# Two-layer backbone kernel: other operand sources, order and issue times in the second MLP products, and other PSUM tiles in the passages

## Chip, cores and metric

The kernel runs on one core of one Trainium2 chip. The metric is the device time of one launch in microseconds. Engines: PE (TensorE, matmuls), DVE (VectorE), ACT (ScalarE), POOL (GpSimd), SP (SyncE, which issues most DMAs here).

## What is computed

Two layers over 1024 latent tokens and a prefix of 256 context tokens, width 1024, all in fp32. Layer 0 mixes tokens with windowed attention, layer 1 with bidirectional gated linear attention (GLA); each is followed by an MLP with 4096 hidden units. Only the latent stream of layer 1 is returned, so layer 1's MLP works on latent tokens alone.

```python
def channel_mlp(h, w_in, w_out):
    return jnp.square(jax.nn.relu(h @ w_in)) @ w_out
...
x_lat = x_lat + m_lat[2] * rms_norm(y_lat, g_post_mix[i])
f_lat = channel_mlp(modulate(x_lat, g_pre_mlp[i], m_lat[3], m_lat[4]), w_mlp_in[i], w_mlp_out[i])
x_lat = x_lat + m_lat[5] * rms_norm(f_lat, g_post_mlp[i])
```

## The kernel before

A product of two fp32 operands is three matmuls: each operand is split into a high and a low part (`split`, L212: an ACT cast, then a DVE subtraction), and `mm3` runs high by high (L229), high by low (L230) and low by high (L231). Both matrices of each MLP product are cut in quarters and multiplied with seven products (numbered 1 to 7) in place of eight; sums and differences of quarters are the operands of products 3 to 7, and part of them are made on DVE.

The first product (`mlp_hidden`, L841) runs over 16 units m of hidden rows: for each it loads two column blocks of `w_mlp_in` (`wi`), runs the seven products into the PSUM tiles `pa`, `pb`, `pc`, takes relu and square on ACT into `h`, and `put` (L944) stores `h` to DRAM (`hd`), 512 KB twice per m; `put_x` (L947) stores the context part `hx` of layer 0 in the same way. `x.ops` holds the split activations, `o1h`, `o1l` to `o7h`, `o7l`.

The second product (`mlp_out`, L991) runs twice, once per half kh of the hidden rows, over seven products k in the order 1, 6, 7, 4, 5, 3, 2, eight units j each, and within these over pairs p of token tiles, five with the context (layer 0), four without (layer 1). `fetch` loads one quarter of hidden rows and one of weights, 256 KB each; for k = 6 it loads two of each, for k = 7 nothing, since `sums` makes product 7's operands out of product 6's loads. `sums` makes the operands on DVE: four sums for k = 6, two for 5, one each for 4 and 3. `apart` splits them into `oh` and `ol`. `product` is one triple of matmuls into `p` (or `px`, context), `read` adds the bank to an accumulator `acc`.

The order around the change is set by hand: a `Timeline` holds closures with due times in nominal us, and runs them by time. A fetch is due 9 us ahead of the sums, these 4.5 us ahead of the matmul, the split 3.6 us. A scheduler then places the instructions of each engine, which run in that order. SP issues its DMAs in order too, so a store that waits for its data holds up the loads behind it. All 128 x 1024 tiles come from one SBUF pool of 45 slots. PSUM has four tiles of one bank (`ps1`) and two of two banks (`ps2`).

Between two stages lies a passage, in which token tiles are normalised, transposed on PE and evicted (`modulated`, L430): ACT and DVE take turns on eight 128 x 128 pieces, into `h` or the raw quarters `q`. While `self.tight` is set, the transposes go into one two-bank tile, since the four single banks hold the accumulators of the second product; the tile's first half is evicted before its second half is transposed. For layer 0 a closure sets it just before the second product; for layer 1 (L1841) it is set at once, when the rest of the passage is still in the timeline. The tile `pb` of the first product lies in the two-bank pool as well.

At the end of GLA, `gla_forward` yields a chunk of 128 tokens, `gla_out` normalises it on ACT, POOL and DVE into `on`, and `turn` (L1500) transposes it into `oT` and splits it. `gate_rows` (L407) makes the row `grow` that the residual is scaled with.

Of the kernel before, what the change touches and what calls it, by code (L numbers as in the profile page):

```python
# [11 lines left out]
F32 = mybir.dt.float32  # L12
# [153 lines left out]
class Backbone:  # L166
# [263 lines left out]
    def modulated(self, xn, l, which, s, dst=(), put=None):  # L430

        nc = self.nc
        G, S = self.pre[l, which]
        both = self.ps2("xt") if self.tight else None
        for q in range(2):
            pt = both[:, 512 * q : 512 * (q + 1)] if self.tight else self.ps1("xt")
            for k in range(4):
                kk = 4 * q + k
                nc.tensor.transpose(pt[:, P * k : P * (k + 1)], xn[:, P * kk : P * (kk + 1)], self.ident)
            h = None if put else self.half("h").rearrange("p (k t) -> p k t", k=4)  # L440
            for k in range(4):
                kk = 4 * q + k
                to = put(kk) if put else h[:, k, :]
                src = pt[:, P * k : P * (k + 1)]
                sc, sh = G[:, s, kk : kk + 1], S[:, s, kk : kk + 1]
                if k % 2 == 0:
                    nc.scalar.activation(to, src, AF.Identity, scale=sc, bias=sh)
                else:
                    nc.vector.tensor_scalar(to, src, sc, sh, ALU.mult, ALU.add)
            for k0, k1, hi, lo in dst:  # L450
                a, b = max(k0, 4 * q), min(k1, 4 * q + 4)
                if a < b:
                    self.split(h[:, a - 4 * q : b - 4 * q, :], hi[:, a - k0 : b - k0, :], lo[:, a - k0 : b - k0, :])
# [377 lines left out]
    def hidden_store(self, ctx):  # L831

        lat = [self.dp.tile([P, 2, 512], F32, name=self.nm("hd")) for _ in range(HID // P)]
        if not ctx:
            return lat, None
        return lat, {
# [4 lines left out]
    def mlp_hidden(self, tl, t0, x, store, g):  # L841
# [102 lines left out]
        def put(m, a):  # L944
            nc.sync.dma_start(store[0][2 * m + a], st[m]["h", a])

# [15 lines left out]
        for m in range(n):  # L962
# [28 lines left out]
    def mlp_out(self, tl, t0, l, pairs, store, split_last, done):  # L991
# [10 lines left out]
        step = mm * np_  # L1002
        order = (1, 6, 7, 4, 5, 3, 2)
        when, t = {}, t0
        for kh in range(2):
            for k in order:
                for j in range(8):
# [8 lines left out]
        def unit(s):  # L1016
            return self.u((P, 2, 512), s=s)

        def hid(dst, m, q):
            r, a = quarter[q]  # L1020
            nc.sync.dma_start(dst, lat_store[2 * m + a][:, r, :])

        def wgt(dst, m, q):
# [4 lines left out]
        def fetch(kh, k, j):  # L1028
            m = 8 * kh + j
            if k == 6:  # L1030
                k3[m], raw[k, m] = unit("k3"), unit("wh")
# [14 lines left out]
        def sums(kh, k, j):  # L1046
            m = 8 * kh + j
            tt = nc.vector.tensor_tensor
            if k == 6:
                a, b, r = k2[m], k3[m], raw.pop((k, m))  # L1050
# [13 lines left out]
        def apart(kh, k, j):  # L1064
            m = 8 * kh + j
            src = k2[m] if k in (1, 6) else k3[m] if k == 7 else raw[k, m]
            hi, lo = (self.u((P, 2, 512), F32R, "o" + x) for x in "hl")
# [49 lines left out]
        def read(kh, k, p):  # L1117
# [11 lines left out]
            if kh == 1:  # L1129
                what = {5: "whole", 3: "half", 2: "whole"}.get(k)  # L1130
                if what:
                    done(what, i, acc[i] if what == "half" else acc.pop(i))

        for kh in range(2):
            for n, k in enumerate(order):
                for j in range(8):
# [9 lines left out]
                    if k != 7:  # L1146
                        tl.at((t if k == 1 else ts) - 9, lambda kh=kh, k=k, j=j: fetch(kh, k, j))
                    if k not in (1, 7, 2):
# [9 lines left out]
                if ctx:  # L1158
                    t = when[kh, k, 0]
                    tl.at(t - 14, lambda kh=kh, k=k: cfetch(kh, k))  # L1160
                    if k in (6, 5, 3):
                        tl.at(t - 7, lambda kh=kh, k=k: csums(kh, k))
                    tl.at(t - 4.6, lambda kh=kh, k=k: capart(kh, k))
        return {k: when[1, k, 0] for k in order}, when[1, 2, 8 - split_last], end

# [349 lines left out]
    def run(self):  # L1515
# [253 lines left out]
        row = self.gate_rows(1, 0, 0)  # L1769
        x3d = [self.dp.tile([P, D], F32, name=f"x3d{i}") for i in range(NL_T)]  # L1770
# [10 lines left out]
        def mlp1_ready(left):  # L1781
# [4 lines left out]
            lat, mixed, wo, x2_in, lambda i: row, lambda i: x3d[i - NC_T], h3, 1,  # L1786
            mixed(NC_T), x2_in(NC_T), mlp1_ready,
        )
# [51 lines left out]

        self.tight = True  # L1841
        ts, tp, te = self.mlp_out(tl, t1, 1, pairs, store, 5, spaced)
# [48 lines left out]
```

## Time and profile before

| | us |
|---|---|
| median of three runs | 2640.89 (2640.38 to 2645.94) |
| profiled execution | 2643.85 |
| its span on the core | 2642.1, mean granted PE clock 0.989 |
| attention and layer 0's mixer | 0 to 640 |
| layer 0, first product | 640 to 1054 |
| layer 0, second product and passage | 1054 to 1470 |
| GLA | 1470 to 1893 |
| output projection of layer 1 | 1893 to 1997 |
| layer 1, first product | 1997 to 2312 |
| layer 1, second product | 2312 to 2633 |

The profile's page gives busy time per engine over the whole span. Where a stage loses time is read from windows of the trace, from the waits of one engine in a window (the instruction that waited, and the one that released it), and from timelines.

### The profile page before, as it was taken

What the parts mean: (1) busy time and instruction counts of PE and PEld (TensorE: products, weight loads), DVE (VectorE), ACT (ScalarE), POOL (GpSimd) and SP (SyncE); (2) the same over time, 40 slices, a digit from 0 to 9 for tenths busy, and PEclk for the clock granted to TensorE, in tenths of its full rate; (3) what the DMA queues carried; (4) which work ended last, traced back from release to release, by engine and by line L of the source; (5) the groups of instructions that cost most, each with busy time, mean ns of one, the idle gap of its engine ahead of it and who ended that gap; (6) DMA issues with size and microseconds to landing.
All of it is one profiled execution on the core that took longest, in us unless ns stands there. A gap on an engine that the chain in (4) does not pass through costs nothing.

```text
span 2642.1 us, 36265 instructions
## 1 busy us (share of the span) xinstructions
PE 2561.1 (97%) x13523; PEld 2124.1 (80%) x13523; DVE 1713.7 (65%) x2663; ACT 1258.3 (48%) x2364; POOL 426.3 (16%) x736
## 2 busy tenths in 40 slices
PE   7999999999999999999998999999998999999998
PEld 6777888888888888788876888888786888878787
DVE  4787766657766665766768534736648444478776
ACT  3325777745644444442335444434435555545333
POOL 0355655411000000000001112212310000000002
PEclk9999999999999999999998999999999999999999
DMA  9221000222455575657245222002222343366464
GB/s 308 93 67 41 4 2 20 70 88 84 144 160 160 173 226 179 223 170 233 100 165 194 96 72 69 25 24 96 88 89 64 112 121 102 125 242 213 169 215 167
DMA packets 223520, 329.75 MB, mean 125 GB/s; under 512 B 23896, under 2 KB 122480, under 8 KB 223344
## 3 DMA queue, kind: packets, MB, share of 16 engines
q1 hardware_dynamic: 220752, 318.00, 37.5%
q0 software_dynamic: 2592, 9.44, 0.9%
q8 instruction: 106, 1.74, 0.3%
q14 instruction: 70, 0.57, 0.1%
HBM read 267.60 MB, written 59.77 MB: 124 GB/s over the span
## 4 chain that ended last, share of the span: by engine, by line
PE 85%; DVE 6%; DMA 4%; ACT 2%; issue 1%; POOL 1%; SPq 1%; DVEq 0%; POOLq 0%; ACTq 0%
PE p L229 7%; PE p L230 7%; PE p L231 7%; PE pa L230 4%; PE pa L231 4%; PE pa L229 4%; PE o L760 3%; PE pt L741 3%; PE y L231 3%; PE y L230 2%; PE y L229 2%; PE rp L229 2%; PE rp L230 2%; PE rp L231 2%; PE pc L229 2%; PE pc L231 2%
## 5 line engine op out<-in xcount | busy, mean ns | idle before, releaser
L230 PE MATMUL p<-ol,oh 128*128 128x512 f32 x896 | 351.0, 392 | 1.5 <-DVE ol L214 1.5
L231 PE MATMUL p<-oh,ol 128*128 128x512 f32 x896 | 346.9, 391 | 0.0
L229 PE MATMUL p<-oh 128*128 128x512 f32 x896 | 332.5, 394 | 6.0 <-DVE acc L1125 4.4
L242 POOL TENSOR_SCALAR rs<-ss 128x1 f32<-128x1 f32 (+1 forms) x78 | 25.4, 326 | 1664.4 <-ACT later L236 1483.7
L229 PEld LDWEIGHTS p<-oh 128*128 128x128 f32 x896 | 169.5, 189 | 43.4 <-issue 4.1
L230 PEld LDWEIGHTS p<-ol,oh 128*128 128x128 f32 x896 | 169.6, 189 | 38.8 <-DVE ol L214 2.8
L231 PEld LDWEIGHTS p<-oh,ol 128*128 128x128 f32 x896 | 169.3, 189 | 35.6 <-issue 0.2
L214 DVE TENSOR_TENSOR ol<-wh,oh 128x1024 fp32r<-128x1024 f32 x128 | 153.7, 1216 | 53.8 <-ACT oh L213 50.8
L311 DVE SCALAR_TENSOR_TENSOR ma<-wm,cT,ma 128x1024 f32<-128x1024 f32 x112 | 148.9, 1361 | 55.1 <-DMA wm<-in_w_mod 55.1
L213 ACT CAST oh<-wh 128x1024 fp32r<-128x1024 f32 x128 | 132.4, 1053 | 107.9 <-PE p L231 46.4
L213 ACT CAST oh<-k 128x1024 fp32r<-128x1024 f32 x96 | 98.5, 1054 | 150.8 <-DMA k<-in_w_mlp_out 56.1
L214 DVE TENSOR_TENSOR wi<-wi,wi 128x512 fp32r<-128x512 f32 x176 | 115.4, 685 | 48.1 <-ACT wi L213 46.4
L932 ACT COPY s<-pa 128x512 f32<-128x512 f32 x96 | 55.9, 583 | 183.6 <-PE pa L231 183.5
L936 DVE TENSOR_TENSOR s<-pc,s 128x512 f32<-128x512 f32 x64 | 43.9, 687 | 145.7 <-ACT s L932 135.9
L708 DVE CUSTOM_DVE_ANT_0 pr<-sc,mask,nsink 128x640 f32<-128x640 f32 (+2 forms) x144 | 108.5, 775 | 43.0 <-PE sc L697 41.1
L214 DVE TENSOR_TENSOR ol<-k,oh 128x1024 fp32r<-128x1024 f32 x96 | 115.5, 1218 | 25.6 <-ACT oh L213 16.9
L713 ACT ACTIVATE pr<-pr,nm 128x640 f32<-128x640 f32 (+2 forms) x160 | 118.5, 742 | 28.1 <-DVE nm L708 25.0
L725 POOL TENSOR_SCALAR pr<-pr,den 128x640 f32<-128x640 f32 (+2 forms) x160 | 117.7, 748 | 36.5 <-PE pt L741 16.9
L213 ACT CAST wi<-wi 128x512 fp32r<-128x512 f32 x176 | 102.3, 614 | 39.4 <-DMA hd<-h 25.1
L231 PE MATMUL y<-woh,ol 128*128 128x512 f32 x288 | 113.1, 393 | 2.8 <-DVE ol L214 2.8
L229 PE MATMUL y<-woh,oh 128*128 128x512 f32 x288 | 114.5, 398 | 0.0
L230 PE MATMUL y<-wol,oh 128*128 128x512 f32 x288 | 113.0, 393 | 0.0
(372 smaller groups left out, 6828.5 us busy)
## 6 DMA issues: line engine op xcount, KB each, us to landing
wm<-in_w_mod SPq DMA_DIRECT2D x96, 512.0 KB, 4.6
wh<-hd SPq DMA_DIRECT2D x160, 256.0 KB, 3.8
wh<-in_w_mlp_out SPq DMA_DIRECT2D x160, 256.0 KB, 4.0
wi<-in_w_mlp_in SPq DMA_DIRECT2D x64, 512.0 KB, 5.6
hd<-h SPq DMA_DIRECT2D x64, 512.0 KB, 3.6
k<-hd SPq DMA_DIRECT2D x64, 256.0 KB, 5.3
k<-in_w_mlp_out SPq DMA_DIRECT2D x64, 256.0 KB, 5.3
x<-in_x SPq DMA_DIRECT2D x16, 512.0 KB, 3.6
```

Source lines behind the costliest of these rows:

```text
L213: self.nc.scalar.copy(hi, src)
L214: self.nc.vector.tensor_tensor(lo, src, hi.bitcast(F32), op=ALU.subtract)
L229: mm(out, a[0], b[0], start=start, stop=False, skip_group_check=onto)
L230: mm(out, a[0], b[1], start=False, stop=False, skip_group_check=onto)
L231: mm(out, a[1], b[0], start=False, stop=stop, skip_group_check=onto)
L311: nc.vector.scalar_tensor_tensor(acc[s], raw, c, acc[s], ALU.mult, ALU.add)
L708: nc.vector.tensor_tensor_reduce(out=like(pr), in0=like(ps[e][:, off:768]), in1=mask, scale=1.0, scalar=self.nsink[:, c0 + e : c0 + e + 1] ...
L713: nc.scalar.activation(pr, pr, AF.Exp, bias=nm[:, e : e + 1], scale=-1.0, accum_out=sums[:, e : e + 1])
L725: nc.gpsimd.tensor_scalar(probs[e], probs[e], den[:, e : e + 1], 0.0, ALU.mult, ALU.add)
L741: nc.tensor.transpose(pt[:, P * j : P * (j + 1)], probs[e][:, P * kt : P * (kt + 1)], self.ident)
L760: nc.tensor.matmul(po[64 * e : 64 * (e + 1), P * i4 : P * (i4 + 1)], self.kv[tile_i // 2][:, tile_i % 2, 256 + HD * g : 256 + HD * (g + 1) ...
L932: nc.scalar.copy(s["s", j], s["pa"])
```

## The change

- Layer 1's `put` now makes operands as well. Per m it writes seven units of 256 KB (h11, h11 - h21, h12, h22, and the operands of products 6, 5 and 3) with four DVE sums. The second product loads an operand as it is (`op`); only the weight side is summed there: two sums for k = 6, one for 4 and 5. Product 7 now has a load of its own, product 6 three.
- Layer 0's first half opens with product 2: its order is 2, 1, 6, 7, 4, 5, 3. The second half and layer 1 keep theirs.
- In the second half of either layer, loads, sums and splits of products 4, 5, 3 and 2 are due 2, 5, 9 and 13 us earlier. The loads of product 6 are due earlier, except in layer 1's first half. The context's loads and splits are due 2 to 2.4 us earlier, its sums 2.
- In `modulated` with `tight` set, both halves are transposed before any eviction.
- In layer 1 `tight` is set by a closure one nominal us before the second product.
- The gate row and the first turned tile are written inside GLA's loop, at the third-last and second-last chunk.

```diff
@@ modulated
+        if self.tight:
+            both = self.ps2("xt")
+            for q in range(2):
+                pts[q] = both[:, 512 * q : 512 * (q + 1)]
+                turn(q)
         for q in range(2):
+            if not self.tight:
+                pts[q] = self.ps1("xt")
+                turn(q)
@@ mlp_hidden, put
+            h = st[m]["h", a]
+            if a == 0:
+                nc.vector.tensor_tensor(h[:, 1, :], h[:, 0, :], h[:, 1, :], op=ALU.subtract)
+                nc.sync.dma_start(store[0][m][:, 0:2, :], h)
+                return
+            nc.sync.dma_start(store[0][m][:, 2:4, :], h)
+            h0, s12, s4 = st[m]["h", 0], self.u((P, 2, 512), s="h"), self.u(s="h")[:, :512]
+            nc.vector.tensor_tensor(s12[:, 0, :], h[:, 1, :], h0[:, 1, :], op=ALU.subtract)
+            nc.vector.tensor_tensor(s12[:, 1, :], s12[:, 0, :], h0[:, 0, :], op=ALU.add)
+            nc.vector.tensor_tensor(s4, h[:, 0, :], s12[:, 0, :], op=ALU.subtract)
+            nc.sync.dma_start(store[0][m][:, 4:6, :], s12)
+            nc.sync.dma_start(store[0][m][:, 6, :], s4)
...
-            tl.at(max(at[m, 4], at[m, 3]) + 8, lambda m=m: put(m, 0))
-            tl.at(max(at[m, 3], at[m, 5]) + 8, lambda m=m: put(m, 1))
+            done = max(at[m, 4], at[m, 3], at[m, 5]) + 8
+            tl.at(done, lambda m=m: put(m, 0))
+            tl.at(done, lambda m=m: put(m, 1))
@@ mlp_out
-        order = (1, 6, 7, 4, 5, 3, 2)
+        made = ctx_store is None
+        last = (1, 6, 7, 4, 5, 3, 2)
+        orders = last if made else (2, 1, 6, 7, 4, 5, 3), last
...
+            if made:
+                if k == 6:
+                    b, a, r = k2[m][:, 1, :], k3[m][:, 1, :], raw.pop((1, m))[:, 1, :]
+                    tt(a, b, a, op=ALU.subtract)
+                    tt(b, a, r, op=ALU.add)
+                else:
+                    r = raw[k, m][:, 1, :]
+                    tt(r, r, k2[m][:, 1, :], op=ALU.subtract)
+                return
...
+        leads = {4: 2.0, 5: 5.0, 3: 9.0, 2: 13.0}
...
-                    ts = t - 4.5
+                    ahead = leads.get(k, 0) if kh else 0
+                    ts = t - 4.5 - ahead
+                    tf = ts - 4.5
                     if k == 6:
-                        ts = when[kh, 1, 0] + (1.35 * j + 0.6) * step
+                        t1 = when[kh, 1, 0]
+                        ts = t1 + (1.35 * j + 0.6) * step
+                        tf = ts - 9 if made and not kh else t1 - 9 + (1.25 * j - (3.5 if kh else 1.5)) * step
...
-                    tl.at(t - 3.6, lambda kh=kh, k=k, j=j: apart(kh, k, j))
+                    tl.at(t - 3.6 - ahead, lambda kh=kh, k=k, j=j: apart(kh, k, j))
@@ run, layer 1
+            if i == NT - 3:
+                row = self.gate_rows(1, 0, 0)
+            if i == NT - 2:
+                ready["o"] = self.turn(on[NC_T])
...
-        self.tight = True
+        tl.at(t1 - 1, lambda: tighten(True))
```

How rows stand, at three places. First SP where layer 0's second product opens (`hd` and `in_w_mlp_out` loads fill one tile in turn; `hc` are the context's stores). Before:

```order
L1021 DMA k_2001_10748<-hd_6196 128x512
L1026 DMA k_2001_10748<-in_w_mlp_out 128x512
L949 DMA hc_6229<-hx_10679 128x128
L949 DMA hc_6233<-hx_10679 128x128
L945 DMA hd_6224<-h_10435 128x1024
L1021 DMA k_2005_10772<-hd_6196 128x512
L1026 DMA k_2005_10772<-in_w_mlp_out 128x512
L1021 DMA wh_10773<-hd_6197 128x512
L1026 DMA wh_10773<-in_w_mlp_out 128x512
L1021 DMA k_2007_10778<-hd_6198 128x512
L1026 DMA k_2007_10778<-in_w_mlp_out 128x512
L949 DMA hc_6231<-hx_10817 128x128
```

Now:

```order
L1052 DMA wh_10748<-hd_6197 128x512
L1060 DMA wh_10748<-in_w_mlp_out 128x512
L975 DMA hc_6229<-hx_10678 128x128
L975 DMA hc_6233<-hx_10678 128x128
L958 DMA hd_6224<-h_10435 128x1024
L1052 DMA wh_10776<-hd_6199 128x512
L1060 DMA wh_10776<-in_w_mlp_out 128x512
L975 DMA hc_6231<-hx_10811 128x128
L1052 DMA wh_10826<-hd_6201 128x512
L1060 DMA wh_10826<-in_w_mlp_out 128x512
L975 DMA hc_6235<-hx_10811 128x128
```

Ahead of the last two `hc` stores four tiles' loads (`k`, `wh`) became two, and each j has one tile, of product 2, in place of three.

Second ACT at the end of GLA, where `grow` is the gate row, `on` the squares of a chunk and `woh` the weight's high part. Before:

```order
L1492 ACTIVATE on_17231,ss_3097_17232<-o_2832_15934 128x256 x2
L1492 ACTIVATE on_17231,ss_3097_17232<-oo_17222 128x256 x2
L213 CAST woh_17246<-wor_17244 128x1024
L1492 ACTIVATE on_17262,ss_3106_17263<-o_2832_15934 128x256 x2
L1492 ACTIVATE on_17262,ss_3106_17263<-oo_17253 128x256 x2
L213 CAST woh_17277<-wor_17275 128x1024
L416 COPY grow_17281<-grow_17282 128x512
L416 COPY grow_17281<-grow_17285 128x512
L213 CAST oh_17328<-oT_17330 128x512
L213 CAST oh_17328<-oT_17337 128x512
```

Now:

```order
L416 COPY grow_17205<-grow_17206 128x512
L416 COPY grow_17205<-grow_17209 128x512
L1556 ACTIVATE on_17238,ss_3100_17239<-o_2832_15934 128x256 x2
L1556 ACTIVATE on_17238,ss_3100_17239<-oo_17229 128x256 x2
L213 CAST woh_17253<-wor_17251 128x1024
L213 CAST oh_17257<-oT_17259 128x512
L213 CAST oh_17257<-oT_17266 128x512
L1556 ACTIVATE on_17285,ss_3113_17286<-o_2832_15934 128x256 x2
L1556 ACTIVATE on_17285,ss_3113_17286<-oo_17276 128x256 x2
L213 CAST woh_17300<-wor_17298 128x1024
L213 CAST oh_17330<-oT_17332 128x512
L213 CAST oh_17330<-oT_17339 128x512
```

The gate's copies moved from behind the last chunk's squares to ahead of the last two chunks, the first tile's casts (`oh`) ahead of the last chunk's.

Third PE in layer 1's passage, between products 1 (`pa`, `o1`) and 2 (`pb`, `o2`). Before:

```order
L230 MATMUL pa_18212<-o1l_17878,wi_3277_18145 128x512
L231 MATMUL pa_18212<-o1h_17877,wi_3277_18145 128x512
L439 MATMUL xt_18161<-ident,xn_18083 128x128 x4
L439 MATMUL xt_18225<-ident,xn_18182 128x128 x4
L229 MATMUL pb_18254<-o2h_18122,wi_3283_18189 128x512
L230 MATMUL pb_18254<-o2l_18123,wi_3283_18189 128x512
L231 MATMUL pb_18254<-o2h_18122,wi_3283_18189 128x512
L229 MATMUL pb_18254<-o2h_18122,wi_3283_18189 128x512
```

Now:

```order
L229 MATMUL pa_18197<-o1h_17861,wi_3261_18129 128x512
L230 MATMUL pa_18197<-o1l_17862,wi_3261_18129 128x512
L231 MATMUL pa_18197<-o1h_17861,wi_3261_18129 128x512
L439 MATMUL xt_18210<-ident,xn_18167 128x128 x4
L229 MATMUL pb_18288<-o2h_18106,wi_3277_18235 128x512
L230 MATMUL pb_18288<-o2l_18107,wi_3277_18235 128x512
L231 MATMUL pb_18288<-o2h_18106,wi_3277_18235 128x512
L229 MATMUL pb_18288<-o2h_18106,wi_3277_18235 128x512
```

The two groups of transposes ahead of `pb`, second half of one tile and first half of the next, became one.

## Rows read from the trace of the kernel before

**Rows 1.** The page, part 1: busy time, share of the span, instructions of each engine.

```profile
PE 2561.1 (97%) x13523; PEld 2124.1 (80%) x13523; DVE 1713.7 (65%) x2663; ACT 1258.3 (48%) x2364; POOL 426.3 (16%) x736
```

**Rows 2.** Windows by stage; columns in the first line.

```profile
core 0: us, PE busy (x) PEld busy (x) DVE busy (x) ACT busy (x) POOL busy (x), PEclk, DMA share, GB/s
1054.00:1090.00 36.00, 29.70 (x117) 22.00 (x116) 26.15 (x34) 10.93 (x13) 0.00 (x0) 0.95 0.99 346
1090.00:1396.00 306.00, 305.96 (x1343) 250.20 (x1342) 213.99 (x253) 118.01 (x127) 0.59 (x2) 1.00 0.49 163
1396.00:1470.00 74.00, 65.06 (x277) 52.27 (x277) 58.30 (x84) 41.93 (x75) 13.97 (x21) 0.91 0.43 150
1996.00:2032.00 36.00, 26.67 (x102) 19.69 (x101) 31.00 (x53) 19.76 (x36) 2.21 (x5) 0.86 0.04 15
2032.00:2312.00 280.00, 279.50 (x1231) 230.70 (x1230) 132.01 (x208) 148.67 (x268) 0.00 (x0) 1.00 0.37 113
2312.00:2642.00 330.00, 315.56 (x1382) 258.48 (x1380) 252.68 (x304) 136.60 (x161) 17.09 (x20) 0.99 0.59 201
```

**Rows 3.** PE and ACT waits, opening of layer 0's second product.

```profile
PE px L229 <- ACT oh L213: 6.3, 5, 2.1
...
ACT oh L213 <- DMA k<-in_w_mlp_out: 22.7, 6, 6.7
```

**Rows 4.** Windows of ten us in that opening, columns as in rows 2.

```profile
1070.00:1080.00 10.00, 7.17 (x29) 5.27 (x30) 6.59 (x9) 3.14 (x3) 0.00 (x0) 1.00 0.99 346
1080.00:1090.00 10.00, 7.88 (x29) 6.05 (x28) 8.88 (x11) 3.58 (x5) 0.00 (x0) 0.83 1.05 393
```

**Rows 5.** SP's waits 1020 to 1095, one issue (start, length); the page's cast and landing time.

```profile
SPq L949 <- ACT hx L894: 20.6, 3, 10.0
...
1050.19 0.79 SPq L949 DMA_DIRECT2D hc<-hx  x2
...
L213 ACT CAST oh<-k 128x1024 fp32r<-128x1024 f32 x96 | 98.5, 1054 | 150.8 <-DMA k<-in_w_mlp_out 56.1
...
k<-in_w_mlp_out SPq DMA_DIRECT2D x64, 256.0 KB, 5.3
```

**Rows 6.** PE waits 1395.8 to 1471; one group of eight transposes (start, length).

```profile
PE xt L439 <- DVE h L449: 4.3, 2, 2.4
PE px L229 <- ACT oh L213: 2.1, 2, 1.5
PE p L230 <- DVE ol L214: 1.5, 1, 1.5
...
1447.64 1.03 PE L439 MATMUL xt<-ident,xn 128*128 128x128 f32 x8
```

**Rows 7.** PE waits 1890 to 1898.

```profile
PE y L231 <- DVE ol L214: 2.8, 1, 2.8
PE oT L1506 <- ACT grow L416: 2.3, 1, 2.3
```

**Rows 8.** Windows with the clock low, columns as in rows 2.

```profile
1420.00:1425.00 5.00, 5.00 (x17) 3.88 (x15) 3.94 (x5) 1.41 (x4) 2.82 (x4) 0.58 0.27 108
1898.00:1903.00 5.00, 5.00 (x16) 3.95 (x15) 1.16 (x2) 0.00 (x0) 0.00 (x0) 0.66 0.01 3
2011.00:2018.00 7.00, 4.79 (x11) 3.80 (x12) 3.15 (x8) 0.49 (x2) 0.00 (x0) 0.52 0.02 4
```

**Rows 9.** PE waits 1996 to 2033.

```profile
PE pb L229 <- DVE q L449: 4.5, 1, 4.5
...
PE pa L229 <- ACT o6h L213: 1.9, 1, 1.9
```

**Rows 10.** DVE groups, second product and hidden stage of layer 1; PE's waits there.

```profile
L1054 DVE TENSOR_TENSOR k<-k,k 128x512 f32<-128x512 f32 x16 | 10.9, 684 | 0.1
...
L936 DVE TENSOR_TENSOR s<-pc,s 128x512 f32<-128x512 f32 x30 | 20.6, 688 | 118.9 <-ACT s L932 109.5 <-PE pc L231 9.2
...
PE p L229 <- DVE acc L1125: 4.4, 3, 2.3
```

More of the change, by code (lines that the diff above doesn't have):

```diff
@@ L433, in modulated, with turn @@
         G, S = self.pre[l, which]
-        both = self.ps2("xt") if self.tight else None
-        for q in range(2):
-            pt = both[:, 512 * q : 512 * (q + 1)] if self.tight else self.ps1("xt")
+        pts = {}
+        def turn(q):
             for k in range(4):
                 kk = 4 * q + k
-                nc.tensor.transpose(pt[:, P * k : P * (k + 1)], xn[:, P * kk : P * (kk + 1)], self.ident)
+                nc.tensor.transpose(pts[q][:, P * k : P * (k + 1)], xn[:, P * kk : P * (kk + 1)], self.ident)
+        if self.tight:
[3 more added lines that the diff above has]
+                turn(q)
+        for q in range(2):
+            if not self.tight:
+                pts[q] = self.ps1("xt")
+                turn(q)
+            pt = pts[q]
             h = None if put else self.half("h").rearrange("p (k t) -> p k t", k=4)
@@ L831, in hidden_store @@
     def hidden_store(self, ctx):
+        if not ctx:
+            return [self.dp.tile([P, 7, 512], F32, name=self.nm("hd")) for _ in range(HID // P // 2)], None
         lat = [self.dp.tile([P, 2, 512], F32, name=self.nm("hd")) for _ in range(HID // P)]
-        if not ctx:
-            return lat, None
         return lat, {
@@ L1002, in mlp_out @@
         step = mm * np_
-        order = (1, 6, 7, 4, 5, 3, 2)
+        made = ctx_store is None
+        last = (1, 6, 7, 4, 5, 3, 2)
+        orders = last if made else (2, 1, 6, 7, 4, 5, 3), last
         when, t = {}, t0
         for kh in range(2):
-            for k in order:
+            for k in orders[kh]:
                 for j in range(8):
@@ L1065, in apart @@
             m = 8 * kh + j
-            src = k2[m] if k in (1, 6) else k3[m] if k == 7 else raw[k, m]
+            src = k3[m] if k == 7 else k2[m] if k == 6 or k == 1 and not made else raw[k, m]
             hi, lo = (self.u((P, 2, 512), F32R, "o" + x) for x in "hl")
@@ L1132, in read @@
                     done(what, i, acc[i] if what == "half" else acc.pop(i))
+        leads = {4: 2.0, 5: 5.0, 3: 9.0, 2: 13.0}
         for kh in range(2):
-            for n, k in enumerate(order):
+            for k in orders[kh]:
                 for j in range(8):
@@ L1159, in mlp_out @@
                     t = when[kh, k, 0]
-                    tl.at(t - 14, lambda kh=kh, k=k: cfetch(kh, k))
+                    t -= leads.get(k, 0) * 0.7 if kh else 0
+                    tl.at(t - 16, lambda kh=kh, k=k: cfetch(kh, k))
                     if k in (6, 5, 3):
-                        tl.at(t - 7, lambda kh=kh, k=k: csums(kh, k))
-                    tl.at(t - 4.6, lambda kh=kh, k=k: capart(kh, k))
-        return {k: when[1, k, 0] for k in order}, when[1, 2, 8 - split_last], end
+                        tl.at(t - 9, lambda kh=kh, k=k: csums(kh, k))
+                    tl.at(t - 7, lambda kh=kh, k=k: capart(kh, k))
+        return {k: when[1, k, 0] for k in last}, when[1, 2, 8 - split_last], end
     def gla_consts(self):
@@ L1786, in run @@
             lat, mixed, wo, x2_in, lambda i: row, lambda i: x3d[i - NC_T], h3, 1,
-            mixed(NC_T), x2_in(NC_T), mlp1_ready,
+            ready["o"], x2_in(NC_T), mlp1_ready,
         )
```

27 lines of the change are left out of this document (22 added, 5 removed).

## Prediction

> **What bounds the kernel now.** I read the page's busy line first: TensorE (PE) is busy 97% of 2642.1 us, VectorE (DVE) 65%, ScalarE (ACT) 48% [rows 1]. A change that leaves the matmuls as they are can only win what is left: PE's idle time and the time it ran at its low clock level. So the second view is the table of windows by stage [rows 2], and the reader should compare two of its columns, the length of a window and PE's instruction count. In the steady stretch of layer 0's second product 306.0 us hold 1343 matmuls, 0.2278 us each. Count times that price, set against the length of another window, is what the window lost, idle and slow clock together:
> - opening of layer 0's second product (1054 to 1090): 117 x 0.2278 = 26.7, lost 9.3 us
> - its tail into layer 1 (1396 to 1470): 277 instructions, 40 of them small transposes, in five groups of eight, each about 0.8 us of PE's time (1.03 with the end of the last one, which overlaps what follows) [rows 6]; 237 x 0.2278 + 4.0 = 58.0, lost 16.0
> - turn to layer 1's output projection (1890 to 1898): two waits make 5.1 us [rows 7], and the clock afterwards is 0.66 for 5 us, in which 16 matmuls ran instead of 22, 1.4 us [rows 8]; lost 6.5
> - passage into layer 1's MLP (1996 to 2032): 102 instructions, 16 of them transposes (1.6 us): 86 x 0.2278 + 1.6 = 21.2, lost 14.8
> - layer 1's second product (2312 to 2642): 1382 x 0.2278 = 314.8, and the last 9 us lie behind the last matmul; lost about 6
> - hidden stage of layer 1 (2032 to 2312): 1231 x 0.2278 = 280.4 for 280 us, lost nothing.
>
> That is some 53 us in five places. Where DVE or ACT is only busy, nothing is won by making it lighter; the waits of PE in those five windows say who must come earlier.
>
> **Opening of layer 0's second product.** Five waits of PE there, 6.3 us, are for ACT's cast of the left operand, and ACT itself waits 22.7 us for DMA, `k<-in_w_mlp_out` [rows 3]. The DMA engines are full (share 0.99 to 1.05, 346 to 393 GB/s) [rows 4], and SP stood up to 10.0 us just before, since a store of `hx` waited for ACT until 1050.2 [rows 5]. Product 1 opens with two loads of 256 KB per j, and product 6's four per j are asked for beside them, six in all. After the change product 2 opens, and each j asks for two: 0.52 MB in a step of 3.4 us (five matmul triples of 0.68) is 154 GB/s, under half of what rows 4 show. In the order of SP the loads of j = 0 and 1 stand ahead of the blocking store, that of j = 2 right behind it, at about 1051; with 5.3 us to land [rows 5] and a cast of 1.05 us [rows 5] it is ready near 1057.5, and PE, starting at 1054, needs it two steps later, at 1060.8. Ready with 3 us to spare. The six loads per j come back later, at product 1: there 2 loads per 3.4 us and 4 per 4.25 us want 401 GB/s for some 27 us, 10.8 MB. At 346 GB/s this takes 31.3 us, 4.3 late; loads are issued 9 us ahead, of which landing and cast leave 2.6, so up to 1.7 us of stall; at 393 GB/s none. Nearest to the row of the same loads I take 1.3 left, gain **8** (5 to 9.3).
>
> The Trainium skill ("DMA: Bandwidth & Descriptors", Where 436 GB/s comes from) puts a core's share of HBM at about 358 GB/s for transfers between HBM and SBUF, which speaks against bringing both products' loads together again. The stretch at 393 GB/s [rows 4] lies above it, so the trace does not bear it out as a ceiling. By 358 the 10.8 MB would take 30.2 us, a stall of 0.6, and the sum would stand as it is within a microsecond.
>
> **Tail of layer 0's second product.** PE waits 4.3 us (twice, 2.4 the longest) for the second half of a transposed tile until DVE has evicted the first half, 2.1 for casts and 1.5 for a low part [rows 6], 7.9 together; most of the other 8.1 is the slow clock after these waits: mean granted 0.58 in 1420 to 1425 [rows 8], mostly the lower of its two levels (1.2 of 2.4 GHz), and once more ten us later. The change writes both halves' transposes in one row of eight before any eviction (the two-bank tile is reserved from the first transpose either way, so nothing is held longer), and the 4.3 goes. The splits of the products 4, 5, 3, 2 are issued 2 to 13 us earlier, so products 3 and 2 should have their parts before the layer's residual work floods ACT and DVE. In the new order on ACT the cast for one of product 2's last steps still stands behind the evictions of two tiles: four pieces of 0.46 us each per tile, some 3.5 us with the waits between. I leave 3 us for it and 1.5 for a second such meeting: gain **11** (6 to 14). The leads cost slots: 13 us ahead is about four steps of 3.4, so four more pairs of high and low parts, eight of 45 slots, at a time when the operands of products 1, 6 and 7 are gone.
>
> **Turn to the output projection.** PE waits 2.3 us for `oT` behind ACT's two copies of the gate row, and 2.8 for the low part, which stands on DVE behind the last tile's output and a weight split [rows 7]. Afterwards the gate row and the first turned tile are written two and one iterations earlier: the copies stand two iterations ahead, and the first tile's cast ahead of the last tile's squares. The first matmul can then run as soon as PE leaves the last chunk; of the 5.1 + 1.4 I leave about 2 us, because the last tile's own chain (POOL's statistics, then DVE) is not shortened. Gain **4.5** (3 to 6.5), with the slow clock after it.
>
> **Passage into layer 1's MLP.** Two waits stand out: 4.5 us for product 2's first matmul until DVE evicted `q`, since the two-bank PSUM tile of the transposes was shared with `pb`, and 1.9 for `o6h` [rows 9]. From 2011 to 2018 the clock is 0.52 [rows 8]: 11 matmuls where 30 would fit, part of it the wait itself. The change leaves the one-bank pool in use for the tiles until just before the second product, so the 4.5 goes and with it the slow stretch after it (about 2). What comes next is `o6h`: it hangs on the last tile's evictions on DVE, which is busy 31.0 of 36 us here [rows 2] and only shifts by what its inputs shift. In the new order the last transposes stand in front of product 2 without a wait in between, so these evictions start about 4.5 us earlier; PE reaches `o6` 6.5 us earlier and finds it some 2 to 3 late. Gain **6** (3 to 9).
>
> **Layer 1's operands.** Removed from the second product: four DVE sums per m of 16, 64 x 0.684 = 43.8 us of the 252.7 that DVE is busy there [rows 10, 2]. Added to the first product: four sums of the same shape per m, 43.8 us on a DVE that is busy 132 of 280 us [rows 2], and three more units of 256 KB written per m, 12.6 MB, 45 GB/s on top of 113. Loads stay seven pairs per m, but product 1 and 6 open with five loads per j, not six. The cover of the sums is the 118.9 us that DVE sat idle ahead of one line there, nearly all for ACT's copies [rows 10]; I cost them at 0, up to 5 if the last two m's sums and stores delay the first loads of the second product, which stand among them on SP. PE waits 4.4 us in the second product for an accumulator's addition on DVE [rows 10], which is what a lighter DVE shortens. Gain **4.5** (0 to 6).
>
> Earlier fetches in layer 0's second half and for the context: 0 (-2 to 2), as that stretch loses next to nothing.
>
> **Sum.** 8 + 11 + 4.5 + 6 + 4.5 = 34. The profiled execution took 2643.85 us, 1.75 outside its span, and gives 2609.9; the median before, 2640.89, lies 3.0 below it, so 2607.
>
> **Rivals.** *Half the gain.* At tail and passage DVE and ACT remain the ones that end last: once the PSUM wait is gone, casts and evictions are next, and the low clock stays, since it follows any wait of some us there. For it: DVE 31.0 of 36 and 58.3 of 74 us busy [rows 2]. Against: the splits move away in time. Tail 5, passage 2, turn 3, opening 6, layer 1 at 1: 17, 2624 (2619 to 2633).
>
> *It doesn't do what it says.* The scheduler places instructions by priorities and may undo the due times: the gain would be under 5 us, 2637 to 2641. Against: the new order does show two loads per j, eight transposes in a row and the gate copies ahead.
>
> *Slower: sums in the hidden stage.* DVE runs in order. The first sum of an m waits for both squared halves from ACT; queued behind it are the low parts of the next weights (`wi`, L214), for which PE waits in its second matmul of a triple. Each m then costs one wait, at worst the 2.74 us of its four sums: 16 x 2.74 = 43.8 lost, 10 more than the gain, 2651. It decides from 34/16 = 2.1 us per m. Against: sums are due 8 us after the last matmul they need, DVE is busy 47% there, and PE lost nothing in that stage.
>
> **Chances.** Forecast (2595 to 2619) 0.64; half 0.19; beyond, below 2595, 0.04; no effect 0.06; slower 0.07. Comparisons of this kernel can tell about 0.2%, 5.3 us, from no change: faster 0.87, same 0.06, slower 0.07. The range 2595 to 2630 leaves out the 0.04 below, the 0.13 of the last two and some 0.03 of the half gain.
>
> **What would show it.** In the opening: PE idle under 2 us from 1054 to 1090, ACT's waits for DMA short, DMA share well under 1 there and near 1 some 27 us later. At the tail: no wait of the second transposes, one or no slow stretch. At the turn: first projection matmul right behind the last chunk. In the passage: `pb` without a wait for `q`, `o6h` with one of 2 to 3 us. In layer 1: DVE near 176 us busy in the hidden stage with PE still full, near 209 in the second product, waits for `acc` mostly gone. Wrong it would be made by a new wait in the hidden stage of layer 1, by PE waits at product 1 of layer 0 of more than 5 us, or by slots: loads waiting for PE's last readers where the leads are largest.

## Result, and the profile after

The changed kernel takes 2615.43 us in the median (2614.03 to 2617.42), the kernel before, timed beside it, 2643.36: a ratio of 0.9895, 95% interval 0.9878 to 0.9912. That is 28 us faster where 34 were forecast; the time lies inside the range (2595 to 2630). The profiled execution took 2614.6 us with a span of 2612.5, against 2643.85 and 2642.1 before, 29.6 us of span.

The page's busy line of the changed kernel, to be read beside [rows 1]: same number of matmuls, 13 us less of PE time (the mean granted clock rose from 0.989 to 0.995), and DVE as busy as before.

```profile
PE 2547.7 (98%) x13523; PEld 2118.3 (81%) x13523; DVE 1718.6 (66%) x2663; ACT 1259.4 (48%) x2364; POOL 421.6 (16%) x736
```

Three pieces of the program tell where the time went. They are cut at PE instructions that both kernels have, read from PE's timeline (for the changed kernel at 1053.08, 1973.19, 2292.52 and 2603.49 us).

| us | before | after | saved | forecast |
|---|---|---|---|---|
| start to layer 0's second product | 1053.9 | 1053.1 | 0.8 | 0 |
| from there to the first matmul of layer 1's MLP (`pa<-o1h`) | 944.9 | 920.1 | 24.8 | 23.5 (8 + 11 + 4.5) |
| to the first matmul of layer 1's second product | 322.9 | 319.3 | 3.6 | 6 |
| to its last matmul | 311.1 | 311.0 | 0.1 | 4.5 |

So the three terms of the first 920 us came out as a sum, the passage gave about half, and the operand sums gave nothing. Each figure is from one profile. By the spread of the changed kernel's code over the other runs (below) the three savings are 22.9 to 24.8, 3.4 to 5.6 and -0.8 to 1.7 us.

The first piece can be cut finer, since both kernels run 13523 PE instructions, and at these cuts the same number of them lies behind in both. The last column has the other runs that keep the changed kernel's code in the stretch.

| stretch | before | after | saved | other runs |
|---|---|---|---|---|
| opening: first 437 PE instructions of layer 0's second product | 109.3 | 102.6 | 6.7 | 102.6 to 104.3 |
| from there to the tail (1406.25 before, 1399.93 now) | 243.1 | 244.3 | -1.2 | 244.4 to 244.9 |
| tail, into layer 1 (to 1534.93, 1515.37) | 128.7 | 115.4 | 13.2 | 115.4, one 115.9 |
| turn (1878.00 to 1905.52, 1858.45 to 1880.20) | 27.5 | 21.8 | 5.8 | 21.7 to 22.0 |

The windows by stage of the changed kernel (columns: length, then busy us and instruction count of PE, PE's weight loads, DVE, ACT, POOL, then the granted clock, the DMA share, GB/s):

```profile
1053.00:1090.00 37.00, 37.00 (x164) 30.37 (x163) 23.30 (x27) 15.26 (x19) 0.00 (x0) 1.00 1.02 357
1100.00:1112.00 12.00, 9.38 (x40) 6.98 (x39) 12.00 (x17) 8.93 (x10) 0.00 (x0) 1.00 0.37 135
1396.00:1446.00 50.00, 47.67 (x228) 38.89 (x227) 42.50 (x64) 35.04 (x66) 11.91 (x18) 1.00 0.51 169
1971.00:2003.00 32.00, 25.05 (x101) 19.65 (x100) 29.13 (x49) 18.66 (x34) 2.44 (x5) 0.86 0.05 17
2003.00:2290.00 287.00, 286.32 (x1256) 236.03 (x1255) 174.03 (x273) 154.11 (x275) 0.00 (x0) 1.00 0.48 155
2290.00:2604.00 314.00, 310.06 (x1356) 254.89 (x1354) 212.92 (x237) 132.44 (x155) 10.37 (x18) 0.99 0.61 207
```

At the 0.2278 us per matmul of [rows 2], the opening (37.0 us, 164 matmuls) now loses nothing, where 36 us lost 9.3 before. What is left of its loss has moved to 1100 to 1112, product 1: 40 matmuls are 9.1 us of 12. DVE is busy in all 12.00 us of that window, and the two waits there are for DVE:

```profile
PE px L229 <- DVE acc L1181: 1.6, 1, 1.6
PE px L230 <- DVE ol L214: 1.0, 1, 1.0
```

At the tail the waits for transposes are gone and the mean granted clock is 1.00; what is left is one wait of 1.5 us and one of 0.8, against the three kinds of [rows 6]:

```profile
PE p L229 <- ACT oh L213: 2.3, 2, 1.5
```

At the turn to the output projection PE goes from GLA's last chunk (`oo`) over four transposes straight into the projection, and the wait for the low part is 0.9 us instead of 2.8 [rows 7] (timeline of PE: start, length, instruction):

```profile
1871.30 0.59 PE L1542 MATMUL oo<-Rf,gq 128*128 128x256 f32 x2
1871.74 0.60 PE L1570 MATMUL oT<-ident,on 128*128 128x128 f32 x4
1872.09 0.47 PE L229 MATMUL y<-woh,oh 128*128 128x512 f32 x1
...
1873.70 0.50 PE L231 MATMUL y<-woh,ol 128*128 128x512 f32 x1 [0.90 <-DVE ol L214]
```

In the passage `pb` waits for nothing any more, as forecast, but `o6` waits longer than in [rows 9], for its high and its low part, and the mean clock is 0.86 as before:

```profile
PE pa L229 <- ACT o6h L213: 3.0, 1, 3.0
PE pa L230 <- DVE o6l L214: 2.0, 1, 2.0
PE pa L229 <- ACT wi L213: 1.8, 1, 1.8
```

In layer 1's second product the waits for `acc` fell from 4.4 to 1.2 us [rows 10], as forecast, but a wait of 2.5 us for a cast is new. It lies at 2309.5 to 2312, in the product's opening, where the DMA engines are full, and the granted clock is 0.66 over the 5 us from 2310 on, part of them at the lower level (1.2 GHz):

```profile
PE p L229 <- ACT oh L213: 2.5, 1, 2.5
PE p L229 <- DVE acc L1181: 1.2, 2, 1.1
...
2305.00:2310.00 5.00, 4.49 (x18) 2.83 (x16) 1.60 (x2) 1.05 (x1) 0.00 (x0) 1.00 1.04 403
2310.00:2315.00 5.00, 2.94 (x7) 2.39 (x8) 3.14 (x4) 3.03 (x3) 0.00 (x0) 0.66 1.06 390
```

### The profile page after: what moved, and what is told of

Its sections match the earlier page's. It is cut to its first block, busy times and chain, and to the rows that moved or that the text cites. A ratio compares the mean times of both kernels' runs of the same rounds, so it can differ in the third digit from the quotient of the medians.

```text
span 2612.5 us, 36352 instructions
## 1 busy us (share of the span) xinstructions
PE 2547.7 (98%) x13523; PEld 2118.3 (81%) x13523; DVE 1718.6 (66%) x2663; ACT 1259.4 (48%) x2364; POOL 421.6 (16%) x736
## 4 chain that ended last, share of the span: by engine, by line
PE 84%; DVE 7%; DMA 4%; issue 2%; ACT 2%; POOL 1%; SPq 0%; DVEq 0%; POOLq 0%; ACTq 0%
PE p L229 7%; PE p L231 6%; PE p L230 6%; PE pa L230 4%; PE pa L229 4%; PE pa L231 4%; PE o L771 3%; PE pt L752 3%; PE y L231 3%; PE y L229 3%; PE y L230 3%; PE rp L230 2%; PE rp L229 2%; PE rp L231 2%; PE pc L229 2%
## 5 line engine op out<-in xcount | busy, mean ns | idle before, releaser
L724 ACT ACTIVATE pr<-pr,nm 128x640 f32<-128x640 f32 (+2 forms) x160 | 118.6, 742 | 27.3 <-DVE nm L719 24.2
L231 PE MATMUL rp<-wgh,al 128*128 128x512 f32 x288 | 112.1, 390 | 0.0
```

The source lines that it names most:

```text
L231: mm(out, a[1], b[0], start=False, stop=stop, skip_group_check=onto)
L724: nc.scalar.activation(pr, pr, AF.Exp, bias=nm[:, e : e + 1], scale=-1.0, accum_out=sums[:, e : e + 1])
```

## Experiments

Twelve kernels were run. Each is read by the three pieces of the first table above, since the time of the whole scatters for a reason outside the change: the start of layer 0's second product lies between 1050.4 and 1057.1 us in these profiles, though the experiments changed nothing ahead of it but the first loads of `u_order`. Where kernels have the same code in a piece, the first piece (920.1 in the changed kernel) came out at 920.1 to 922.0 in seven, the second at 317.3 to 319.5 in nine, the third at 309.4 to 311.9 in seven; a difference counts where it leaves these bounds. All medians stand against a kernel before of 2643.4 to 2644.2 us.

| kernel | median us | first piece | second | third |
|---|---|---|---|---|
| changed kernel | 2615.43 | 920.1 | 319.3 | 311.0 |
| u_order | 2620.56 | 924.8 | 319.3 | 311.0 |
| u_leads | 2622.88 | 930.4 | 317.6 | 308.7 |
| u_halves | 2625.99 | 931.3 | 319.5 | 311.9 |
| u_gate | 2618.77 | 926.8 | 317.3 | 309.4 |
| u_tight | 2615.72 | 921.5 | 320.1 | 311.6 |
| u_ops | 2618.38 | 922.0 | 320.0 | 312.7 |
| x_double | 2611.23 | 921.6 | 318.0 | 310.5 |
| x_nosum6 | 2614.19 | 917.9 | 318.3 | 311.4 |
| v_l1open | 2615.34 | 920.9 | 317.6 | 311.4 |
| v_l1leads | 2615.76 | 921.2 | 319.3 | 309.1 |
| v_all | 2613.10 | 921.9 | 319.4 | 309.7 |
| v_pool | 2608.01 | 920.7 | 318.3 | 304.4 |

**Which product opens (u_order).**

```diff
-        orders = last if made else (2, 1, 6, 7, 4, 5, 3), last
+        orders = last, last
```

> The changed kernel, but layer 0's second product opens with product 1 as before. Theory (opening: loads wait): the loss of about 10 us between the first matmul of the product and 40 us later comes back and the small stall of 3.4 us some 50 us after the start goes; net 6 to 8 us slower than the changed kernel, near 2622, ratio to the kernel before 0.992. Rival (the earlier fetches of product 6 alone cure it): under 2 us slower.

The first piece is 2.8 to 4.7 us longer. PE waits at the opening for a cast again, once for 3.3 us, but far less than the 6.3 us in five waits of [rows 3]. The opening takes 107.1 us here, 102.6 in the changed kernel and 109.3 before, so the order is worth 4.5 us, less than the theory said and more than the rival. The other 2.2 are left to the other edits there (load times of product 6 and of the context), which were not tried singly.

```profile
PE px L229 <- ACT oh L213: 3.3, 1, 3.3
PE px L230 <- DVE ol L214: 0.6, 1, 0.6
```

**What the rest of the opening waits for (x_nosum6).** The kernel leaves out the 32 DVE sums of product 6 in layer 0's first half; loads stay.

```diff
             a, b, r = k2[m], k3[m], raw.pop((k, m))
+            if kh == 0:
+                return
```

> The changed kernel without the 32 sums of product 6 in layer 0's first half; so products 6 and 7 of that half work on the unsummed quarters, while all loads stay. Theory (the stall near 1100 to 1112 is DVE, which is busy without a gap there): the 3.3 us of that stretch fall under 1 us. Rival (loads of products 1 and 6 together, as the prediction had it): the stall stays at 2 to 4 us.

First the 35 us around the stall in the changed kernel, then the same stretch, some 3 us later by the clock, without the sums: DVE falls from 34.5 to 20.6 us busy, the DMA share and GB/s are the same, and PE's 140 matmuls become 151. The wait left is 0.2 us.

```profile
1080.00:1115.00 35.00, 32.38 (x140) 25.76 (x140) 34.52 (x47) 17.12 (x20) 0.00 (x0) 1.00 0.73 269
```

```profile
1083.00:1118.00 35.00, 34.68 (x151) 27.62 (x150) 20.59 (x21) 19.33 (x22) 0.00 (x0) 1.00 0.73 271
...
PE px L229 <- ACT oh L213: 0.2, 1, 0.2
```

So the stall that the prediction had put down to loads (1.3 us at 346 GB/s) is DVE's: ten splits, 28 of the 32 sums and the context's sums and split stand there almost without a gap.

**The tail (u_leads, u_halves).**

```diff
-        leads = {4: 2.0, 5: 5.0, 3: 9.0, 2: 13.0}
+        leads = {}
```

> The changed kernel with all leads of products 4, 5, 3, 2 in the second half set to zero. Theory (tail: splits late behind the residual work): PE's waits for casts and low parts come back at the end of layer 0's second product, with a stretch at the low clock; 5 to 9 us slower than the changed kernel, near 2622. Rival (the transposes alone cured the tail): under 2 us slower.

The first piece is 8.4 to 10.3 us longer; the tail takes 127.5 us, 12.0 more than in the changed kernel, and the stretch ahead of it 242.6, 1.7 less, so the leads also cost something there. What PE waits for in the tail is not what the theory said, though: it is mostly the transposes (`xt`), 6.8 us for evictions of the tile before on DVE (`h`) and 2.4 for an accumulator's addition; the casts and low parts are a small rest. For loads the list of the change is not right: those of products 4, 5, 3 and 2 were due 13.5 us ahead of the matmul and are now due 9 us and the lead ahead (9 without a lead), that is 2.5 us later for product 4 and 0.5, 4.5 and 8.5 earlier for 5, 3 and 2. In this run they come 4.5 us later than in the kernel before, so it does not bring that kernel's order back; PE's waits are for evictions, not for loads.

```profile
PE xt L439 <- DVE h L460: 6.8, 2, 4.4
PE xt L439 <- DVE acc L1181: 2.4, 1, 2.4
PE p L230 <- DVE ol L214: 1.3, 1, 1.3
...
1410.00:1420.00 10.00, 6.92 (x23) 5.51 (x23) 7.77 (x14) 6.62 (x14) 2.80 (x4) 0.68 0.39 125
```

```diff
         for q in range(2):
             if not self.tight:
                 pts[q] = self.ps1("xt")
-                turn(q)
+            turn(q)
```

(and the call of `turn` ahead of the loop taken out)

> The changed kernel with the second half of a tile transposed after the first half's evictions, as before, where one two-bank tile is used. Theory: the two waits of transposes for the eviction (4.3 us before) come back, with up to 4 us of low clock: 4 to 8 us slower than the changed kernel, near 2621. Rival (with the leads in place PE has other work around these transposes): under 2 us slower.

The first piece is 9.3 to 11.2 us longer, though the leads are in place; the tail takes 125.1 us, 9.7 more. One wait of 2.6 us for the first half's eviction is back, with the low clock behind it (0.70), and later a projection of layer 1 waits 3.9 us, for a cast of `gv`. Neither the kernel before nor the changed one has that second wait.

```profile
PE rp L229 <- ACT gv L1283: 3.9, 1, 3.9
PE xt L439 <- DVE h L459: 2.6, 1, 2.6
...
1425.00:1435.00 10.00, 6.74 (x25) 5.14 (x24) 8.27 (x15) 8.73 (x18) 2.34 (x4) 0.70 0.83 252
```

Undone singly the two edits cost 21.7 us in the tail (12.0 and 9.7), where both together won 13.2. So these costs can't be added up: each undoing also makes waits that the kernel before did not have (6.8 us for evictions without the leads, 4.3 in [rows 6]; the 3.9 for `gv`).

**The turn (u_gate).** The gate row and the first turned tile go back behind the loop.

```diff
-            if i == NT - 3:
-                row = self.gate_rows(1, 0, 0)
-            if i == NT - 2:
-                ready["o"] = self.turn(on[NC_T])
...
+        row = self.gate_rows(1, 0, 0)
```

> The changed kernel with the gate row and the first turned tile written after the end of the GLA loop, as before. Theory: the waits of 2.3 and 2.8 us at the turn to the output projection come back and the low clock after them (1.4 us): 3 to 5 us slower than the changed kernel, near 2619. Rival (PE had to wait for the last tile in any case): under 1.5 us slower.

The first piece is 4.8 to 6.7 us longer, the turn takes 27.5 us as before, and both waits of [rows 7] are back, 2.3 and 2.3 us.

```profile
PE oT L1570 <- ACT grow L416: 2.3, 1, 2.3
PE y L231 <- DVE ol L214: 2.3, 1, 2.3
```

**The passage (u_tight).**

```diff
-        tl.at(t1 - 1, lambda: tighten(True))
+        tighten(True)
```

> The changed kernel with the two-bank tiles in use from the start of layer 1's passage, as before. Theory: PE waits 4 to 5 us for product 2's bank in the passage again; 4 to 7 us slower than the changed kernel, near 2621. Rival (the evenly spread evictions of o6 end last in any case): the wait only moves from o6h and o6l to pb, under 2 us slower.

The second piece is 320.1 us, 0.6 to 2.8 over that of the kernels that have the changed kernel's code there: a part of the 3.6 at most. `pb` waits for `q` again, 1.8 us, not the 4.5 of [rows 9], since the transposes of the two halves now stand together; PE's wait for `o6h` is 1.2 us shorter than in the changed kernel, and the one of 2.0 for `o6l` is gone. So the rival is nearer: most of the wait moves.

```profile
PE pb L229 <- DVE q L460: 1.8, 1, 1.8
PE pa L229 <- ACT o6h L213: 1.8, 1, 1.8
```

**Layer 1's operands (u_ops, x_double).** In `u_ops` layer 1 stores `h` and sums as before, with the rest of the change (`made = False` in layer 1, `hidden_store` and `put` as before).

> The changed kernel with layer 1's operand sums left in the second product and h stored as before. What was forecast (4.5 us from a lighter DVE in the second product): 3 to 6 us slower than the changed kernel, near 2620, with waits for acc of some 4 us back. Rival, which the trace of the changed kernel suggests (PE lost 5.4 us in that product both before and after): within 2 us of the changed kernel, DVE near 250 us busy in the product, and the early stall at its opening still there, since that one is the loads'.

The third piece is 312.7 us, 0.8 to 3.3 over that of the kernels with the new operands. DVE is at 246.5 us again, but the 4 us of waits for `acc` do not come back (1.4 us, 1.2 in the changed kernel), so a lighter DVE alone does not explain that they shortened. The early stall, which the rival had put down to the loads, is gone: the first 86 PE instructions of the product take 20.0 us, 24.2 in the changed kernel. A single wait of 3.9 us stands at the turn to product 6 of the second half, from 2470.6, where DVE's sums of that product end last under the new load times; with the slow clock behind it the stretch is 5.9 us longer. So the new operands save 5.9 us there and cost 4.3 at the opening.

```profile
PE p L229 <- ACT oh L213: 3.9, 1, 3.9
PE p L229 <- DVE acc L1180: 1.4, 2, 0.8
...
2293.00:2607.00 314.00, 308.56 (x1351) 253.83 (x1350) 246.52 (x295) 132.28 (x154) 9.72 (x16) 0.99 0.58 200
```

`x_double` repeats three of the sums of layer 1's first product and makes the last a third time, 43.8 us more of DVE.

```diff
-            nc.vector.tensor_tensor(s12[:, 0, :], h[:, 1, :], h0[:, 1, :], op=ALU.subtract)
-            nc.vector.tensor_tensor(s12[:, 1, :], s12[:, 0, :], h0[:, 0, :], op=ALU.add)
-            nc.vector.tensor_tensor(s4, h[:, 0, :], s12[:, 0, :], op=ALU.subtract)
+            for n in range(2):
+                nc.vector.tensor_tensor(s12[:, 0, :], h[:, 1, :], h0[:, 1, :], op=ALU.subtract)
+                nc.vector.tensor_tensor(s12[:, 1, :], s12[:, 0, :], h0[:, 0, :], op=ALU.add)
+                for _ in range(n + 1):
+                    nc.vector.tensor_tensor(s4, h[:, 0, :], s12[:, 0, :], op=ALU.subtract)
```

> The changed kernel with the operand sums of layer 1's first product made twice: three sums repeated and one more, four more of 0.68 us per m, 43.8 us of DVE in all. Theory (DVE has room in the hidden stage): PE's lost time there stays under 2.5 us, within 2 us of the changed kernel; DVE near 215 of 287 us busy. Rival (DVE's order holds up the weights' low parts): at least 0.5 us per m, 8 us slower or more.

DVE is busy 212 of 287 us in the hidden stage, and PE still runs 1257 matmuls in 287 us, against 1256 in the changed kernel. The slower rival of the prediction is out: 2.7 us more of DVE per m cost nothing.

```profile
2001.00:2288.00 287.00, 286.32 (x1257) 235.92 (x1257) 212.05 (x332) 154.01 (x275) 0.00 (x0) 1.00 0.46 154
```

Its median is 4 us below the changed kernel's. That is not put down to the sums: in the profiles it is 3.1 us of span, and 2.7 of them lie ahead of layer 0's second product, where the two kernels are the same.

**Layer 1's opening and a faster version (v_l1open, v_l1leads, v_all, v_pool).** `v_l1open` moves product 6's loads and sums.

```diff
                         ts = t1 + (1.35 * j + 0.6) * step
+                        if made and not kh:
+                            ts = t1 + 12.0 + step * j
```

> The changed kernel, with product 6's loads and sums in layer 1's first half due some 10 us later (sums at 12 us after the product's start and every 2.72 us, loads 9 us ahead of them). Theory (the 2.7 us stall and the clock after it there come from five loads per j that stand among each other, at 358 to 403 GB/s): PE's loss in the first 40 us of layer 1's second product falls from 4.4 to under 1.5 us; 2 to 4 us faster than the changed kernel. Rival (slots or the casts of product 1 end last): it stays over 3 us.

No gain; the theory fell for this edit alone. The stall is as long as in the changed kernel (2.7 us for casts), but here SP's queue shows why: it issues nothing from 2286.9 to 2293.1, waiting 5.9 us with the store of the last m (L963) for DVE's first sum, and the DMA share from 2290 to 2300 is 0.58. A longer wait, 15.0 us with a store of the m before (L965), had ended at 2278.2 (SP's two waits, two issues, the window, PE's wait):

```profile
SPq L965 <- ACT h L906: 15.0, 1, 15.0
SPq L963 <- DVE h L962: 7.4, 2, 5.9
...
2286.50 0.43 SPq L1060 DMA_DIRECT2D k<-in_w_mlp_out  x1
2293.11 0.32 SPq L963 DMA_DIRECT2D hd<-h  x1
...
2290.00:2300.00 10.00, 10.00 (x46) 8.29 (x45) 7.50 (x9) 5.94 (x8) 0.00 (x0) 1.00 0.58 175
...
PE p L229 <- ACT oh L213: 2.7, 2, 2.5
```

The changed kernel's own stall is another case. There SP stands 12.6 us with the store of the m before, but only 1.5 with the last one's, and the DMA engines are full in the same ten us:

```profile
SPq L965 <- ACT h L906: 12.6, 1, 12.6
SPq L963 <- DVE h L962: 2.9, 2, 1.5
...
2290.00:2300.00 10.00, 10.00 (x46) 8.26 (x44) 9.01 (x12) 5.32 (x7) 0.00 (x0) 1.00 1.01 371
```

`v_l1leads` keeps the leads to layer 0.

```diff
-                    ahead = leads.get(k, 0) if kh else 0
+                    ahead = leads.get(k, 0) if kh and not made else 0
```

> The changed kernel with the leads of products 4, 5, 3, 2 in layer 0 alone. Theory (in layer 1 no work of a next layer stands behind the tail, so the leads only crowd DVE there: with all leads off the loss in layer 1's second product was 3.3 us, with them 5.4): 1 to 3 us faster than the changed kernel. Rival (they cover the output's norms): same or up to 3 us slower.

The third piece is 309.1 us, with `u_leads` (308.7) the lowest yet but just below the scatter; the waits for `acc` are gone. The medians do not tell it from the changed kernel.

`v_all` joins both, and spreads product 6's sums in layer 0's first half (1.6 for 1.35).

> The changed kernel with both edits just named, and product 6's sums in layer 0's first half spread over 1.6 steps per j instead of 1.35. Theory: 2 to 3 us from layer 1's opening, 1 to 2 from its leads, 1 to 2 from layer 0's stall near 1100: 4 to 7 us faster than the changed kernel, near 2609.5, ratio to the kernel before 0.987. Rival (each stall moves on to the next reader): within 2 us of the changed kernel.

2613.10 us, 2.3 below the changed kernel: short of the theory's 4 to 7 and just outside the rival's 2. Spreading the sums gained nothing (first piece 921.9), and the stall in layer 1's opening stayed (one wait of 2.3 us, SP 6.6 us on the last m's store).

`v_pool` is `v_l1leads` with `v_l1open`, and the stores of the last two m go to POOL's queue.

```diff
+            q = nc.gpsimd if m >= n - 2 else nc.sync
...
-                nc.sync.dma_start(store[0][m][:, 0:2, :], h)
+                q.dma_start(store[0][m][:, 0:2, :], h)
```

(the other three stores likewise)

> The changed kernel with leads in layer 0 alone, product 6's loads and sums in layer 1's first half later (as in the run that moved them alone), and the stores of the last two m of layer 1's first product issued by POOL instead of SP. Theory (with the loads moved, SP stands 5.9 us on the store of the last m, ahead of product 1's loads, so the stall at the product's opening stays): with that store off SP the loss of the first 40 us falls from 4.4 to under 1 us, and with the leads gone the whole second product of layer 1 loses under 1.5 us instead of 5.4; 3 to 5 us faster than the changed kernel, ratio to the kernel before near 0.988. Rival (the rate of the DMA engines sets it, not SP): the loss in the first 40 us stays over 3 us.

The third piece falls to 304.4 us, 6.6 less than in the changed kernel, 4.7 less than in `v_l1leads` and 5.3 less than in `v_all`, which differs from it in this piece by the stores' queue alone. PE waits for nothing in it (the one wait left lies ahead of it, in the first product). The DMA engines run at 402 and 410 GB/s around the product's start (2293.7), so with the later loads it was SP's queue and not the engines' rate that held PE.

```profile
PE pa L229 <- ACT s L944: 0.7, 1, 0.7
...
2288.00:2298.00 10.00, 9.89 (x44) 8.19 (x45) 6.02 (x7) 8.03 (x12) 1.07 (x2) 1.00 1.05 402
2298.00:2308.00 10.00, 10.00 (x46) 8.29 (x45) 9.86 (x14) 4.28 (x5) 1.08 (x2) 1.00 1.04 410
...
2291.00:2599.00 308.00, 307.48 (x1357) 254.28 (x1355) 214.25 (x240) 132.22 (x156) 15.49 (x20) 1.00 0.60 204
```

2608.01 us, ratio to the kernel before 0.9861 (0.9844 to 0.9877): 36 us faster than the kernel before and 7 faster than the changed kernel, more than the 3 to 5 expected. Whether the later loads of `v_l1open` are needed in it was not tried. So for the changed kernel itself, with five loads per j and full DMA engines, it stays open whether the queue or the rate held PE.

## Why the prediction was right, and where it was not

- **Opening, 8 us.** Not one wait in the first 37 us, as forecast: the two loads per j that product 2 needs come first, an order worth 4.5 us (`u_order`). That the DMA share would fall well under 1 there was wrong (1.02 at 357 GB/s: product 1's and 6's loads now run ahead into this window). What is left is 2.9 us at product 1, so 6.4 of 9.3 were won (6.7 by the finer cut), and 1.6 more stayed than the sum had left, and for another reason: DVE, not the loads. The step that failed is the one that costed the return of the six loads per j by GB/s alone; the DVE row of the same window (8.88 of 10 us busy in [rows 4]) was on the table and not used.
- **Tail, 11 us.** 13.2 came, and 1.2 were lost ahead of it, where the leads cost 1.7 (`u_leads`). Of the two stalls of 3 and 1.5 us that were left in the sum, 2.3 us came. The order of causes was different: without the leads it is the PSUM tile of the transposes that runs late, more than the casts.
- **Turn, 4.5 us.** The waits fell from 5.1 to 0.9 us, the turn is 5.8 us shorter, and undoing the edit costs 5.7 of them. Right; the 2 us left in the sum were too many.
- **Passage, 6 us.** 3.6 came (3.4 to 5.6 by the spread). The forecast had PE find `o6` 2 to 3 us late; it is 5.0 (3.0 and 2.0). The step that failed is that the last tile's evictions would start 4.5 us earlier, because its transposes would stand ahead of product 2. Its last four transposes still run behind the start of product 2, at 1992.97 us, 2018.32 before: 25.35 earlier, and 25.3 was PE ahead already when the passage began, so nothing was won on them (PE's timeline, before and now, below). The move to one-bank tiles, to which the term was put down, costs 0.6 to 2.8 when undone; that the transposes stand together already shortens the wait for `pb` from 4.5 to 1.8.

```profile
2018.32 0.60 PE L439 MATMUL xt<-ident,xn 128*128 128x128 f32 x4
...
1992.97 0.66 PE L439 MATMUL xt<-ident,xn 128*128 128x128 f32 x4 [0.16 <-DVE q L460]
```

- **Layer 1's operands, 4.5 us.** 0.1 came; undoing the operands costs 0.8 to 3.3. The sums were free where they went, in the first product (`x_double`). The waits for `acc` shrank by 3.2 us; that the lighter DVE did it is not shown, since with the old operands they stay at 1.4 and DVE's sums cost a wait of 3.9 for a cast instead (`u_ops`). The step that failed most is the cost "0, up to 5 if the last two m's sums and stores delay the first loads", of which 0 was taken: the opening loses 4.3 us more than with the old operands, 2.5 of wait and the slow clock behind it. The prediction named the stores among the first loads and gave them no price. Whether they did it by holding SP's queue or by filling the DMA engines is shown only where the loads come later (the queue), and stays open for the changed kernel.
- **Sum.** 34 forecast, 28 in the medians, 29.6 in the spans; the missing parts are the last two terms and 1.6 of the opening, against 2.2 more at the tail and 1.3 more at the turn. So the sum came nearer than its terms: what those two gave beyond the forecast hid part of what layer 1 did not give, and that is luck. None of the rivals happened as a whole; of "half the gain" the reason held for the passage (a cast and a low part end last, 5.0 us), and the size for layer 1's operands (0.1, its 1). The Trainium skill's 358 GB/s per core ("DMA: Bandwidth & Descriptors", Where 436 GB/s comes from) is passed again here: 402 and 410 GB/s over 10 us each in `v_pool`.

## What to carry to other kernels

When a change moves arithmetic from one stage to another, follow its stores and the queue they share: in `v_l1open` a store that waits for its data stopped the next stage's first loads for 5.9 us, and moving such stores to an idle queue was worth 5.3 us (`v_pool` against `v_all`). Cost the return of a burst on every engine it needs, splits and sums too, not on the DMA rate alone. And before dividing a gain among parts, undo them one by one and see whether the costs add up: two edits at one place cost 21.7 us undone singly, where both together had won 13.2. Such an undoing can make waits of its own.

## What was not expected of the hardware

The same code ran with different times: layer 0's second product began between 1050.4 and 1057.1 us in thirteen profiles of kernels that are alike up to there (but for the first loads of one), 6.7 us apart, more than most single terms here. Yet a piece cut at common instructions can repeat closely: the tail took 115.4 us in ten of the eleven kernels with its code. And one core's DMA engines moved 410 GB/s over 10 us of loads and stores of 256 and 512 KB.
